# Group 0's feed-forward with seven block products for eight, its weight sums on GpSimd and by DRAM

## The chip, the cores and the metric

The kernel runs on one core of one Trainium2 chip. The metric is the device time of one execution in microseconds, median of the runs shown; less is better. A core has TensorE (PE; PEld is its weight load), VectorE (DVE), ScalarE (ACT), GpSimd (POOL) and SyncE (SP), which issues most DMAs. Each engine works through a queue of its own in order and waits on semaphores.

## The reference, cut to what matters

One encoder layer over two request groups: 1024 new frames of one stream (positions 0 to 1023) and 32 frames of a running stream with 256 cached positions. Model width 1024, feed-forward width D_FF = 2816, all in float32:

```python
    h = x * (1 + sc1) + sh1
    mq, mk, mv, mo, mi, mf, fq, fk, fv, ff, gu, gv = jnp.split(h @ w_in, split_at, axis=-1)
    hm = ...   # mLSTM matrix memory, 4 heads, chunks of 64
    hf = ...   # forgetting attention (FoX), 8 heads of 64, causal
    hg = ...   # gMLP spatial gate
    mix = jnp.concatenate([hm, hf, hg], axis=-1) @ w_o
    x = _layer_norm(ALPHA * x + (1 + g1) * mix, ln1_g, ln1_b)
    h = x * (1 + sc2) + sh2
    y = (jax.nn.silu(h @ w_gate) * (h @ w_up)) @ w_down
    x = _layer_norm(ALPHA * x + (1 + g2) * y, ln2_g, ln2_b)
```

Outputs are both groups' `y`, the new keys, values and forget logs, and the mLSTM states.

## The kernel before, in words

**Columns.** Activations stand feature-major: 128 features a partition, tokens along the columns. The 1056 tokens are cut into two column groups, GN = (512, 544): group 0 is the first 512 prompt tokens, group 1 the other 512 and the 32 sample tokens.

**Precision.** A float32 value is split into a high part (a cast to fp32r on ACT, names ending in `hi` or `h`) and the remainder (a subtraction, mostly on DVE, `lo` or `l`). `gemm` takes three matmuls for each 128 x 128 block: high by high, low activations by high weights, high by low (lines L130, L131, L132). `weights` loads 512 KB as `raw`, casts (L117) and subtracts (L118). There are three `raw` buffers and three of `whi` and `wlo` (RAW, WB).

**Stages.** (1) Input projections and attention for group 0 (to about 350 us); (2) output projection and first LayerNorm of group 0; (3) the feed-forward of group 0, in which `mixers` weave FoX query tiles 4 to 7, mLSTM chunks and the sample stream's attention (about 440 to 835 us); (4) output projection and LayerNorm of group 1; (5) the feed-forward of group 1 (to about 1290 us) and the second LayerNorms. Feed-forward tiles j = 0 to 21 hold 128 of the 2816 features, each with a gate and an up half; GROUPS gathers them in runs of 3, 3, 4, 4, 4, 4, after each of which `down` multiplies by w_down.

**A tile of group 0** (`up`): two weight splits, two products of 8 blocks x 3 matmuls x 512 columns, SiLU as exp, ln, exp on ACT (L1296 to L1298), two products on DVE (L1299, L1300), then the split into `acth` (L1301) and `actl` (L1302).

**A tile of group 1** from SJ = 3 to 20 (`sup`): a Winograd form. The gate and up weights' four quarter blocks (two halves of the 1024 input features for each of gate and up) and the two column halves make a 2 x 2 by 2 x 2 block product, which takes seven block products (u1, x, w3, w4, own, and so on) in place of eight, with sums of weight blocks and sums of activation blocks. Activation sums are made once in `sup_operand` from the LayerNorm's result, stored to DRAM as `dh`. Weight sums come by DRAM too: `sums` copies blocks of w_gu to `dp[j]` (SP's queue) and adds others to it with an accumulating DMA issued by POOL (L1320), a tile ahead. Partial results are put together on DVE (L1395 to L1409).

**Order.** Within an engine a tile scheduler sets the order from the program's dependencies; `weave` and `issue_after` shape it. The FoX score scaling `fox_p` (L924) goes to DVE or ACT by FP. mLSTM scores (L746) take two matmuls of K = 128 per chunk against `mqb`, which holds the queries of two heads with zeros in the other half (memset by POOL, L719). `ln1_pairs` forms the first LayerNorm of group 0 two feature blocks at a time, in `sil`, a tag with two buffers.

## Time and profile before

| | us |
|---|---|
| runs | 1345.75 (1345.29 to 1346.57) |
| profiled execution | 1344.9 (span and whole) |
| PE busy | 1324.0 |
| DVE busy | 989.1 |
| ACT busy | 655.8 |
| POOL busy | 231.9 |

Busy time is the union of an engine's instructions. A PE row's length includes its pipeline, so a matmul's rate is read from the distance of starts. A window line gives, for a stretch of the execution, each engine's busy time and count.

### The profile page before, as it was taken

What the parts mean: (1) busy time and instruction counts of PE and PEld (TensorE: products, weight loads), DVE (VectorE), ACT (ScalarE), POOL (GpSimd) and SP (SyncE); (2) the same over time, 40 slices, a digit from 0 to 9 for tenths busy, and PEclk for the clock granted to TensorE, in tenths of its full rate; (3) what the DMA queues carried; (4) which work ended last, traced back from release to release, by engine and by line L of the source; (5) the groups of instructions that cost most, each with busy time, mean ns of one, the idle gap of its engine ahead of it and who ended that gap; (6) DMA issues with size and microseconds to landing.
All of it is one profiled execution on the core that took longest, in us unless ns stands there. A gap on an engine that the chain in (4) does not pass through costs nothing.

```text
span 1344.9 us, 25607 instructions
## 1 busy us (share of the span) xinstructions
PE 1324.0 (98%) x9684; PEld 1208.3 (90%) x9684; DVE 989.1 (74%) x2091; ACT 655.8 (49%) x1305; POOL 231.9 (17%) x263
## 2 busy tenths in 40 slices
...
GB/s 362 207 299 154 150 204 186 174 131 207 181 195 257 191 136 130 117 163 126 115 121 116 110 104 82 217 175 112 205 231 154 228 148 225 139 175 131 89 79 67
DMA packets 119450, 221.73 MB, mean 165 GB/s; under 512 B 18580, under 2 KB 62768, under 8 KB 119328
## 3 DMA queue, kind: packets, MB, share of 16 engines
...
q14 instruction: 46, 0.38, 0.1%
HBM read 188.13 MB, written 51.85 MB: 178 GB/s over the span
## 4 chain that ended last, share of the span: by engine, by line
PE 68%; DVE 4%; DMA 1%; ACT 1%; issue 1%; DVEq 0%; ACTq 0%
PE up_g L130 6%; PE up_g L132 6%; PE up_g L131 6%; PE dn_g L130 4%; PE dn_g L132 4%; PE dn_g L131 4%; PE sup_u L132 3%; PE sup_u L131 3%; PE sup_u L130 3%; PE wo_g L131 2%; PE wo_g L132 2%; PE wo_g L130 2%; PE sup_g L132 2%; PE sup_g L131 2%; PE sup_g L130 2%; PE fox_t L943 2%
## 5 line engine op out<-in xcount | busy, mean ns | idle before, releaser
L130 PE MATMUL up_g<-tm_ah,up_whi 128*128 128x512 f32 (+1 forms) x384 | 140.0, 365 | 0.0
L131 PE MATMUL up_g<-tm_al,up_whi 128*128 128x512 f32 (+1 forms) x384 | 140.0, 365 | 0.0
L132 PE MATMUL up_g<-tm_ah,up_wlo 128*128 128x512 f32 (+1 forms) x384 | 139.7, 364 | 0.0
L1368 ACT CAST sup_whi<-sup_raw 128x1024 fp32r<-128x1024 f32 x54 | 56.1, 1048 | 89.3 <-PE dn_u L131 43.9
L130 PEld LDWEIGHTS up_g<-tm_ah,up_whi 128*128 128x128 f32 x384 | 72.3, 188 | 11.1 <-DVE tm_al L1246 0.4
L132 PEld LDWEIGHTS up_g<-tm_ah,up_wlo 128*128 128x128 f32 x384 | 72.3, 188 | 11.1
L131 PEld LDWEIGHTS up_g<-tm_al,up_whi 128*128 128x128 f32 x384 | 72.3, 188 | 10.7
L916 ACT ACTIVATE fox_p<-fox_s,fox_fmx 128x384 f32<-128x384 f32 (+2 forms) x96 | 55.2, 579 | 53.0 <-DVE fox_fmx L914 41.2
L1199 DVE SCALAR_TENSOR_TENSOR wo_z<-dn_g,start_mod,wo_z 128x512 f32<-128x512 f32 (+4 forms) x120 | 60.3, 521 | 22.6 <-PE dn_g L132 22.0
L118 DVE TENSOR_TENSOR up_wlo<-up_raw,up_whi 128x1024 fp32r<-128x1024 f32 x50 | 65.2, 1305 | 15.0 <-ACT up_whi L117 13.7
L1369 DVE TENSOR_TENSOR sup_wlo<-sup_raw,sup_whi 128x1024 fp32r<-128x1024 f32 x54 | 68.0, 1263 | 10.7 <-ACT sup_whi L1368 10.7
L117 ACT CAST up_whi<-up_raw 128x1024 fp32r<-128x1024 f32 x50 | 52.4, 1048 | 47.2 <-PE up_g L131 23.9
L130 PE MATMUL dn_g<-up_acth,dn_whi 128*128 128x512 f32 (+2 forms) x200 | 73.5, 368 | 0.8 <-DVE wo_z L1199 0.8
L132 PE MATMUL dn_g<-up_acth,dn_wlo 128*128 128x512 f32 (+2 forms) x200 | 73.3, 366 | 0.0
L131 PE MATMUL dn_g<-up_actl,dn_whi 128*128 128x512 f32 (+2 forms) x200 | 72.8, 365 | 0.0
L948 ACT CAST fox_pth<-fox_t 128x512 fp32r<-128x512 f32 (+1 forms) x80 | 41.6, 542 | 59.2 <-PE fox_t L943 57.5
L117 ACT CAST dn_whi<-dn_raw 128x1024 fp32r<-128x1024 f32 (+1 forms) x44 | 42.7, 971 | 51.7 <-PE up_g L131 16.0
L911 DVE TENSOR_REDUCE fox_fmx<-fox_s 128x1 f32<-128x384 f32 (+2 forms) x96 | 52.8, 553 | 16.3 <-PE fox_s L908 15.0
L949 DVE TENSOR_TENSOR fox_ptl<-fox_t,fox_pth 128x512 fp32r<-128x512 f32 (+1 forms) x80 | 49.9, 631 | 15.9 <-ACT fox_pth L948 15.6
L118 DVE TENSOR_TENSOR dn_wlo<-dn_raw,dn_whi 128x1024 fp32r<-128x1024 f32 (+1 forms) x44 | 49.5, 1125 | 10.4 <-ACT dn_whi L117 9.5
L402 PE MATMUL tm_g<-tm_whi,start_h1h 128*128 128x256 f32 (+1 forms) x192 | 55.3, 288 | 0.7 <-DVE tm_traw L477 0.7
L1320 POOL DMA_DIRECT2D start_dp<-w_gu x19 | 19.8, 1067 | 209.0 <-DMA start_dp<-w_gu 209.0
...
## 6 DMA issues: line engine op xcount, KB each, us to landing
up_raw<-w_gu SPq DMA_DIRECT2D x50, 512.0 KB
ada_late<-w_ada SPq DMA_DIRECT2D x28, 512.0 KB
dn_raw<-w_dn SPq DMA_DIRECT2D x28, 512.0 KB
sup_raw<-w_gu SPq DMA_DIRECT2D x20, 512.0 KB
start_dp<-w_gu SPq DMA_DIRECT2D x19, 512.0 KB
start_dp<-w_gu POOLq DMA_DIRECT2D x19, 512.0 KB, 8.0
wo_raw<-w_o SPq DMA_DIRECT2D x18, 512.0 KB
sup_raw<-start_dp SPq DMA_DIRECT2D x18, 512.0 KB
```

The lines of the kernel that those rows point to most:

```text
L117: nc.scalar.copy(hi[:, :w], raw[:, :w])
L118: (eng or nc.vector).tensor_tensor(lo[:, :w], raw[:, :w], f(hi[:, :w]), ALU.subtract)
L130: nc.tensor.matmul(ps, hi, xh(k), start=start and k == 0, stop=False)
L131: nc.tensor.matmul(ps, hi, xl(k), start=False, stop=False)
L132: self.lastmm = nc.tensor.matmul(ps, lo, xh(k), start=False, stop=stop and k == n - 1)
L402: nc.tensor.matmul(ps[:, :ncol], xh, hi, start=k == 0, stop=False)
L911: nc.vector.tensor_reduce(mxs[:, x:x + 1], s[:, :w], AX.X, ALU.max, negate=True)
L916: nc.scalar.activation(pr[:, lo:hi], banks[x][:, :hi - lo], AF.Exp, bias=mxs[:, 0:1], accum_out=sums[:, x:x + 1])
L949: nc.vector.tensor_tensor(pl[:, :e], ps[:, :e], f(ph[:, :e]), ALU.subtract)
L1199: self.lastz = self.nc.vector.scalar_tensor_tensor(z[:, m, x:y], ps[:, x - a:y - a], g[i], z[:, m, x:y], ALU.mult, ALU.add)
L1368: nc.scalar.copy(h, x)
L1369: tt(l, x, f(h), ALU.subtract)
```

## The change

- Tiles 3 to 17 of group 0 (S0 = 3 up to the last run) use `sup0`, seven block products of 4 blocks x 3 matmuls x 256 columns, 84 matmuls for 48 of 512. Their weight sums `dp` are formed by two additions on POOL, stored to DRAM through POOL's queue, and read by group 1's `sup` for the same tile, so `sums` is left for tiles 18 to 20 alone. The split of w4 (the sums) subtracts on POOL.
- `sup_operand(0, ...)` makes the activation sums between tiles 0, 1 and 2, the block sums on POOL, from group 0's LayerNorm result, which `ln1_pairs` now stores. One block of four is written over the own activations; `own_again` reloads it before tile 18.
- FoX query tiles 4 to 7 are scaled by ACT (FP).
- mLSTM scores use K = 64 rows, four matmuls in two banks (`sts`), and one multiplication of 512 becomes two of 256; `mqb`, its loads and memsets go.
- Smaller buffers: fox `p` for query tiles 4 to 7 sized per tile, pools `pn` and `p2` closed and reopened elsewhere, a DMA scratch of 4096.

```diff
-FP = (0, 0)
+FP = (0, 1)
...
 SJ = 3
+S0 = 3
 TS = 1
...
-        qb = t([P, 2, 2, P], "mqb")
-        nc.gpsimd.memset(qb, 0.0)
-        for a in range(2):
-            r = slice(64 * a, 64 * a + 64)
-            self.load(qb[r, :, a, :L], self.dmqk[r, 0:2, o:o + L])
...
-        st = self.t(self.pss, [P, 512], F32, "s")
+        sts = [self.t(p, [P, 512], F32, x) for p, x in ((self.pss, "s"), (self.pt, "t"))]
         for i in range(2):
-            nc.tensor.matmul(st[:L, 256 * i:256 * i + 256].rearrange("p (a q) -> p a q", a=2)[:, :, :L],
-                             qk[:, 2 + i, :L], qb[:, i, :, :L], start=True, stop=True)
-        nc.vector.tensor_tensor(w[:L, :, :L], st[:L].rearrange("p (h q) -> p h q", h=4)[:, :, :L], w[:L, :, :L], ALU.mult)
+            for a, st in enumerate(sts):
+                r = slice(64 * a, 64 * a + 64)
+                nc.tensor.matmul(st[:L, P * i:P * i + L], qk[r, 2 + i, :L], qk[r, i, :L], start=True, stop=True)
+        for a, st in enumerate(sts):
+            wa = w.rearrange("p (i a) q -> p i a q", a=2)[:L, :, a, :L]
+            nc.vector.tensor_tensor(wa, st[:L, :256].rearrange("p (i q) -> p i q", i=2)[:, :, :L], wa, ALU.mult)
...
-            pr = t([P, W], F32, "p", 4)
+            pr = t([P, W], F32, "p", 4) if i < 4 else t([P, n], F32, f"p{i}", 1)
...
+            self.store(self.dh[0][:, k:k + 2, sl], h)
...
-        if i < FF:
+        if i < FF - TS:
             with self.tc.issue_after(self.lastload.ins):
                 self.store(self.dp[i], blocks(i)[:, 2:3].to_broadcast([P, 2, 512]))
-        if SJ <= i - 1 < FF:
+        if GROUPS[-1][0] <= i - 1 < FF - TS:
             self.nc.gpsimd.dma_start(self.dp[i - 1], blocks(i - 1)[:, 0:4:3], accum_op=ALU.add)
...
+        else:
+            new = lambda tag, w: [self.t(self.px, [P, 4, w], F32R, tag + x, 1) for x in "hl"]
+            q, r, own = new("tx", 2 * n), new("ty", n), [x[0][n][:, 0:4, :n] for x in (self.hh, self.hl)]
+            self.T[c] = [[x[:, :, i:i + n] for x in q] for i in (0, n)] + [r, own]
...
+            tt = (nc.vector if c else nc.gpsimd).tensor_tensor
             tt(y[:, b], y[:, b], x[:, b], ALU.subtract)
             tt(x[:, b], x[:, a], x[:, b], ALU.subtract)
             tt(x[:, a], y[:, b], x[:, a], ALU.add)
             tt(y[:, a], x[:, a], y[:, a], ALU.subtract)
-            for z, (h, l) in zip((x, y), self.T):
+            for z, (h, l) in zip((x, y), pair) if c else ((x, q), (y[:, a], r)):
                 nc.scalar.copy(h[:, k], z)
-                tt(l[:, k], z, f(h[:, k]), ALU.subtract)
+                nc.vector.tensor_tensor(l[:, k], z, f(h[:, k]), ALU.subtract)
...
+        x = self.t(self.px, [P, 1024], F32, "dp", 1).rearrange("p (k n) -> p k n", k=4)
+        self.load(x, self.dh[c][:, 0:4, b])
+        for i, z in enumerate(("w2h", "w2l")):
+            y = f(self.t(self.px, [P, 512], F32R, z, 1)).rearrange("p (k n) -> p k n", k=2)
+            self.load(y, self.dh[c][:, 4 + 2 * i:6 + 2 * i, b])
+            k = slice(2 * i, 2 * i + 2)
+            nc.vector.tensor_tensor(y, y, x[:, k], ALU.subtract)
+            h, l = own
+            nc.scalar.copy(h[:, k], y)
+            nc.vector.tensor_tensor(l[:, k], y, f(h[:, k]), ALU.subtract)
...
+    def sup0(self, j, act, pool):
+        self.phase = "sup"
+        nc = self.nc
+        tt, pp = nc.vector.tensor_tensor, nc.gpsimd.tensor_tensor
+        hh, hl = self.hh[0], self.hl[0]
+        ah, al = act[j] = [self.t(pool, [P, 512], F32R, x, 5) for x in ("acth", "actl")]
+        raw = [self.t(self.wp, [P, 1056], F32, "raw", RAW)[:, :1024] for _ in range(2)]
+        for i in range(2):
+            self.load(raw[i], self.d["w_gu"][j][:, i * 1024:(i + 1) * 1024])
+        lo, hi = slice(0, 512), slice(512, 1024)
+        dp = self.t(self.px, [P, 1024], F32, "dp", 1)
+        pp(dp[:, hi], raw[1][:, lo], raw[1][:, hi], ALU.add)
+        pp(dp[:, lo], raw[1][:, lo], raw[0][:, lo], ALU.add)
+        self.store(self.dp[j].rearrange("p b n -> p (b n)"), dp, nc.gpsimd)
+
+        def split(h, l, x, eng):
+            nc.scalar.copy(h, x)
+            eng(l, x, f(h), ALU.subtract)
+            return [(h[:, k * P:k * P + P], l[:, k * P:k * P + P]) for k in range(x.shape[1] // P)]
+
+        big = lambda x, eng=tt: split(*(self.t(self.wp, [P, 1056], F32R, y, WB)[:, :1024] for y in ("whi", "wlo")), x, eng)
+        w1 = big(raw[0])
+        tt(raw[0][:, lo], raw[0][:, lo], dp[:, hi], ALU.add)
+        tt(raw[0][:, hi], raw[0][:, hi], raw[0][:, lo], ALU.add)
+        w3 = big(raw[0])
+        w4 = big(dp, pp)
+        w2 = split(*(self.t(self.px, [P, 512], F32R, x, 1) for x in ("w2h", "w2l")), raw[1][:, hi], tt)
+        own = lambda t, k0: tuple(lambda k, x=x: x[t][:, k0 + k, :256] for x in (hh, hl))
+        com = lambda i: tuple(lambda k, x=x: x[:, k] for x in self.T[0][i])
+        a, b = slice(0, 256), slice(256, 512)
+        banks = []
+
+        def prod(w, x):
+            if len(banks) % 2 == 0:
+                banks.append(self.t(self.pg, [P, 512], F32, "g"))
+                ps = banks[-1][:, a]
+            else:
+                banks.append(None)
+                ps = banks[-2][:, b]
+            self.gemm(ps, w, slice(0, P), *x)
+            return ps
+
+        u1 = self.t(self.p2, [P, 272], F32, "tmp", 4)[:, :256]
+        x = self.t(self.p2, [P, 544], F32, "sil", 2)[:, :512]
+        uv = self.t(self.px, [P, 512], F32, "uv", 1)
+        nc.scalar.copy(u1, prod(w1[:4], own(0, 0)))
+        tt(x[:, a], prod(w1[4:], own(0, 4)), u1, ALU.add)
+        tt(uv[:, a], u1, prod(w3[:4], com(0)), ALU.subtract)
+        tt(uv[:, b], prod(w4[4:], com(1)), uv[:, a], ALU.add)
+        tt(x[:, b], prod(w3[4:], own(256, 4)), uv[:, b], ALU.add)
+        s = self.t(self.p2, [P, 544], F32, "sil", 2)[:, :512]
+        nc.scalar.activation(s, x, AF.Exp, scale=-1.0)
+        nc.scalar.activation(s, s, AF.Ln, bias=self.one)
+        nc.scalar.activation(s, s, AF.Exp, scale=-1.0)
+        tt(s, x, s, ALU.mult)
+        two = lambda y: y.rearrange("p (t n) -> p t n", t=2)
+        tt(two(uv), prod(w4[:4], com(3)).unsqueeze(1).to_broadcast([P, 2, 256]), two(uv), ALU.add)
+        tt(uv[:, a], prod(w2, com(2)), uv[:, a], ALU.add)
+        nc.vector.scalar_tensor_tensor(uv, uv, -1.0, s, ALU.mult, ALU.mult)
+        nc.scalar.copy(ah, uv)
+        self.lastact = tt(al, uv, f(ah), ALU.subtract)
+
+    def own_again(self):
+        self.phase = "sup"
+        for k in range(4):
+            r = self.t(self.p2, [P, 272], F32, "tmp", 4)[:, :256]
+            self.load(r, self.dh[0][:, k, 256:])
+            h, l = (x[0][256][:, k, :256] for x in (self.hh, self.hl))
+            self.nc.scalar.copy(h, r)
+            self.nc.vector.tensor_tensor(l, r, f(h), ALU.subtract)
...
-        self.nsum = SJ
+        self.nsum = GROUPS[-1][0]
...
+        s6 = ExitStack()
+        self.px = self.pool("px0", ctx=s6)
+        operand = self.sup_operand(0, range(4))
...
+                if S0 <= j < GROUPS[-1][0]:
+                    self.sup0(j, act, pa)
+                    continue
+                if j == GROUPS[-1][0]:
+                    self.own_again()
                 weave(self.up(0, j, act, pa, WIDE if 0 < j < GROUPS[-1][0] else MM[0]))
+                if j < S0:
+                    with tc.issue_after(self.lastact.ins):
+                        next(operand, None)
+                        next(operand, None)
...
+                s6.close()
+                s4.close()
+                self.pn = self.pool("pn", side="right")
...
-    nc = bacc.Bacc("TRN2", target_bir_lowering=False, num_devices=1)
+    nc = bacc.Bacc("TRN2", target_bir_lowering=False, num_devices=1, dynamic_dma_scratch_size=4096)
```

Where the orders of instructions differ, first on DVE near the first changed tile. Before, tile 4's two weight splits (`up_wlo`) among FoX scores (`fox_`) and evacuations of the down product (`wo_z`):

```order
L118 TENSOR_TENSOR up_wlo_8345<-up_raw_8342,up_whi_8344 128x1024
L914 TENSOR_TENSOR fox_fmx_6224<-fox_fmx_6224 128x1
L1199 SCALAR_TENSOR_TENSOR wo_z_883_4902<-dn_g_8290,start_mod_153,wo_z_883_4902 128x512
L919 TENSOR_TENSOR fox_fsm_6225<-fox_fsm_6225 128x1
L920 RECIPROCAL fox_fsm_6225<-fox_fsm_6225 128x1
L1199 SCALAR_TENSOR_TENSOR wo_z_883_4902<-dn_g_8301,start_mod_153,wo_z_883_4902 128x512
L924 TENSOR_SCALAR fox_p_6226<-fox_p_6226,fox_fsm_6225 128x640
L756 TENSOR_TENSOR mlstm_mkw_6245<-mlstm_t_6242,start_col_178 128x256
L118 TENSOR_TENSOR up_wlo_8351<-up_raw_8348,up_whi_8350 128x1024
L911 TENSOR_REDUCE fox_fmx_6247<-fox_s_6250 128x1
L910 TENSOR_TENSOR fox_s_6254<-fox_s_6254,start_maskneg_130 128x128
L911 TENSOR_REDUCE fox_fmx_6247<-fox_s_6254 128x1
```

Now, tile 3: the third sum (`sup_raw<-sup_raw,sup_dp`), w2's split, the fourth sum and w3's split.

```order
L1402 TENSOR_TENSOR sup_raw_8232<-sup_raw_8232,sup_dp_8236 128x512
L910 TENSOR_REDUCE fox_fmx_6012<-fox_s_6019 128x1
L1397 TENSOR_TENSOR sup_w2l_8255<-sup_raw_8233,sup_w2h_8254 128x512
L1403 TENSOR_TENSOR sup_raw_8232<-sup_raw_8232 128x512
L913 TENSOR_TENSOR fox_fmx_6012<-fox_fmx_6012 128x1
L1397 TENSOR_TENSOR sup_wlo_8247<-sup_raw_8232,sup_whi_8246 128x1024
L918 TENSOR_TENSOR fox_fsm_6013<-fox_fsm_6013 128x1
L919 RECIPROCAL fox_fsm_6013<-fox_fsm_6013 128x1
L119 TENSOR_TENSOR dn_wlo_8367<-dn_raw_8364,dn_whi_8366 128x768
L1014 TENSOR_TENSOR foxs_s_6100<-foxs_s_6100,start_smask_139 128x32
L1017 TENSOR_REDUCE foxs_fmx_6110<-foxs_s_6100 128x1
L948 TENSOR_TENSOR fox_ptl_6036<-fox_t_6031,fox_pth_6035 128x384
```

Tile 3's split of w1 (`sup_wlo_8241`) stands earlier in the same queue, the splits and sums of 512 are new, and all of them stand among FoX, sample-stream (`foxs_`) and down work.

On POOL, before, the mixing stage has only the mLSTM work (`mqb` zeros, a column of ones, the output gate's bias):

```order
L719 MEMSET mlstm_mqb_6185 128x512
L724 MEMSET mlstm_mv_1087_6189 128x4
L735 TENSOR_TENSOR mlstm_mo_6192<-mlstm_mo_6192,start_rowp_176 128x256
L719 MEMSET mlstm_mqb_6482 128x512
L724 MEMSET mlstm_mv_1169_6486 128x4
L735 TENSOR_TENSOR mlstm_mo_6489<-mlstm_mo_6489,start_rowp_176 128x256
L719 MEMSET mlstm_mqb_6747 128x512
L724 MEMSET mlstm_mv_1241_6751 128x4
L735 TENSOR_TENSOR mlstm_mo_6754<-mlstm_mo_6754,start_rowp_176 128x256
L719 MEMSET mlstm_mqb_7012 128x512
L724 MEMSET mlstm_mv_1313_7016 128x4
L735 TENSOR_TENSOR mlstm_mo_7019<-mlstm_mo_7019,start_rowp_176 128x256
```

Now, the first changed tiles on POOL, each of them two additions, the store of the sums and w4's split:

```order
L1391 TENSOR_TENSOR sup_dp_8236<-sup_raw_8233 128x512
L1392 TENSOR_TENSOR sup_dp_8236<-sup_raw_8233,sup_raw_8232 128x512
L92 DMA start_dp_14_70<-sup_dp_8236 128x1024
L1397 TENSOR_TENSOR sup_wlo_8251<-sup_dp_8236,sup_whi_8250 128x1024
L1391 TENSOR_TENSOR sup_dp_8482<-sup_raw_8479 128x512
L1392 TENSOR_TENSOR sup_dp_8482<-sup_raw_8479,sup_raw_8478 128x512
L92 DMA start_dp_15_71<-sup_dp_8482 128x1024
L720 MEMSET mlstm_mv_1168_6491 128x4
L1397 TENSOR_TENSOR sup_wlo_8497<-sup_dp_8482,sup_whi_8496 128x1024
L1391 TENSOR_TENSOR sup_dp_8616<-sup_raw_8613 128x512
```

The next tile's sums stand behind w4's split of the tile before, and write the one `dp` buffer that the store reads. 

On PE, the place where tile 4's first product (`up_g`) follows the first down product (`dn_g`), before:

```order
L130 MATMUL dn_g_8329<-up_acth_8084,dn_whi_8314 128x512
L131 MATMUL dn_g_8329<-up_actl_8085,dn_whi_8314 128x512
L132 MATMUL dn_g_8329<-up_acth_8084,dn_wlo_8315 128x512
L130 MATMUL up_g_8354<-tm_ah_4651,up_whi_8344 128x512
L131 MATMUL up_g_8354<-tm_al_4652,up_whi_8344 128x512
L132 MATMUL up_g_8354<-tm_ah_4651,up_wlo_8345 128x512
```

And the same place now:

```order
L131 MATMUL dn_g_8465<-up_acth_8138,dn_whi_8450 128x512
L132 MATMUL dn_g_8465<-up_actl_8139,dn_whi_8450 128x512
L133 MATMUL dn_g_8465<-up_acth_8138,dn_wlo_8451 128x512
L131 MATMUL sup_g_8507<-tm_ah_4651,sup_whi_8486 128x256
L132 MATMUL sup_g_8507<-tm_al_4652,sup_whi_8486 128x256
L133 MATMUL sup_g_8507<-tm_ah_4651,sup_wlo_8487 128x256
```

Each weight block still takes three passes, of 256 columns where there were 512.

58 lines of the change are left out of this document (35 added, 23 removed).

## The prediction

> **What bounds the kernel now.** I read the page's busy line first, then its chain, then windows over the stage that the change touches and, as a yardstick, over the stage of group 1 that already uses seven products.
>
> ```profile
> PE 1324.0 (98%) x9684; PEld 1208.3 (90%) x9684; DVE 989.1 (74%) x2091; ACT 655.8 (49%) x1305; POOL 231.9 (17%) x263
> PE 68%; DVE 4%; DMA 1%; ACT 1%; issue 1%; DVEq 0%; ACTq 0%
> ```
>
> TensorE (PE) is busy 98% of 1344.9 us: only 20.9 us are idle, and the chain that ended last is mostly PE. So time is won only by giving PE less to do, and lost only where another engine becomes late enough to stop it. The windows show how much room the others have (columns: stretch and length, then busy us and count of PE, weight load, VectorE (DVE), ScalarE (ACT), GpSimd (POOL), then granted clock, DMA share and GB/s).
>
> ```profile
> 430.00:476.30 46.30, 46.27 (x301) 40.12 (x301) 34.51 (x72) 30.58 (x65) 11.42 (x11) 1.00 0.66 191
> 476.30:671.00 194.70, 194.70 (x1061) 161.90 (x1060) 142.98 (x302) 95.30 (x201) 4.88 (x10) 1.00 0.48 134
> 671.00:861.20 190.20, 190.20 (x1068) 162.75 (x1067) 131.35 (x267) 93.47 (x192) 11.29 (x9) 1.00 0.42 125
> 950.00:1000.00 50.00, 49.18 (x394) 48.96 (x393) 44.59 (x86) 33.28 (x71) 16.50 (x18) 1.00 0.84 221
> 965.00:990.00 25.00, 24.18 (x193) 23.96 (x192) 24.17 (x50) 18.31 (x37) 3.10 (x3) 1.00 0.90 223
> 990.00:1015.00 25.00, 23.88 (x186) 23.34 (x185) 18.21 (x38) 11.03 (x19) 3.10 (x3) 1.00 0.90 232
> 1050.00:1250.00 200.00, 200.00 (x1594) 199.94 (x1593) 172.01 (x307) 101.11 (x145) 9.27 (x9) 1.00 0.61 173
> 1165.00:1190.00 25.00, 25.00 (x201) 25.00 (x201) 23.77 (x45) 14.43 (x21) 1.03 (x1) 1.00 0.72 215
> 476.28 0.69 DVE L1302 TENSOR_TENSOR up_actl<-up_sil,up_acth 128x512 fp32r<-128x512 f32 x1
> 493.29 0.69 DVE L1302 TENSOR_TENSOR up_actl<-up_sil,up_acth 128x512 fp32r<-128x512 f32 x1
> 643.81 0.68 DVE L1302 TENSOR_TENSOR up_actl<-up_sil,up_acth 128x512 fp32r<-128x512 f32 x1
> ```
>
> In group 0's mixing stage PE is full and DVE is at 73% and 69% of the two halves. L1302 ends a tile: 476.28 is tile 2, 493.29 tile 3, 643.81 tile 10, so the first half holds eight of the changed tiles (3 to 10) and the second seven. In group 1's seven-product stage DVE is at 86% with PE at 100%, and for 25 us (1165 to 1190) DVE reaches 95% (23.77 of 25.00) while PE loses nothing. The change spends DVE and POOL time to save PE time, so the question is whether DVE fits.
>
> **PE's gain.** A changed tile takes 84 matmuls of 256 columns for 48 of 512. PE's rows give starts, not the pipelined lengths:
>
> ```profile
> 464.10 0.40 PE L130 MATMUL up_g<-tm_ah,up_whi 128*128 128x512 f32 x1
> 464.33 0.39 PE L131 MATMUL up_g<-tm_al,up_whi 128*128 128x512 f32 x1
> 440.26 0.28 PE L130 MATMUL up_g<-tm_ah,up_whi 128*128 128x256 f32 x1
> 440.85 0.28 PE L132 MATMUL up_g<-tm_ah,up_wlo 128*128 128x256 f32 x1
> ```
>
> 512 columns start 0.233 us apart over a longer row; 256 columns are (440.85 − 440.26)/5 = 0.118 us apart, each with its own weight load. So 48 × 0.233 = 11.19 us become 84 × 0.118 = 9.95 us: 1.24 us a tile, **−18.6 us** over 15.
>
> **PE's mLSTM scores.** Two fp32 matmuls of 256 columns a chunk (the trace shows four passes) become four of 128 columns on half the rows.
>
> ```profile
> 494.53 0.59 PE L746 MATMUL mlstm_s<-mlstm_mqb,mlstm_mqk 128*128 128x256 f32 x2
> 496.73 0.60 PE L746 MATMUL mlstm_s<-mlstm_mqb,mlstm_mqk 128*128 128x256 f32 x2
> ```
>
> Two passes take 0.60 with 0.38 us of pipeline, so four take about 0.86 us. Eight passes of half the columns take the same if they run one behind the other, and half if two row halves run side by side: between 0 and −0.43 us for each of 8 chunks, 0 to −3.4. No row of before runs on half the array, so I take the middle, **−1.7 us**. [...]
>
> **DMA relief in group 1.** Sixteen pairs of 512 KB copies that form weight sums leave 850 to 1250 us.
>
> ```profile
> 955.60 5.58 DMA start_dh<-lna_tmp
> 992.39 11.37 DMA dn_raw<-w_dn
> ```
>
> These two steps of the chain lie where the DMA engines are 90% busy, and PE loses 0.82 and 1.12 us there (windows 965 and 990). So the gain is 0 to −1.9; I take **−1.0**. Total gain of PE: 18.6 + 1.7 + 1.0 = 21.3 us, to 1323.6.
>
> **DVE's bill.** The prices:
>
> ```profile
> L118 DVE TENSOR_TENSOR up_wlo<-up_raw,up_whi x50: 1207/1225/3076, 421.9 to 977.7; 128x1024 fp32r<-128x1024 f32 x50
> L1300 DVE TENSOR_TENSOR up_sil<-up_g,up_sil x21: 411/692/693, 444.7 to 818.9; 128x512 f32<-128x512 f32 x17, 128x256 f32<-128x256 f32 x4
> L1369 DVE TENSOR_TENSOR sup_w2l<-sup_w,sup_w2h 128x512 fp32r<-128x512 f32 x13 | 8.9, 686 | 0.0
> L924 DVE TENSOR_SCALAR fox_p<-fox_p,fox_fsm x32: 542/682/1049, 457.3 to 816.2; 128x640 f32<-128x640 f32 x8, 128x768 f32<-128x768 f32 x8, 128x896 f32<-128x896 f32 x8, 128x1024 f32<-128x1024 f32 x8
> 836.36 0.69 DVE L1058 TENSOR_TENSOR wo_z<-wo_z,up_pv 128x512 f32<-128x512 f32 x1 [2.21 <-ACT up_pv L1057]
> 836.97 0.74 DVE L1199 SCALAR_TENSOR_TENSOR wo_z<-dn_g,start_mod,wo_z 128x512 f32<-128x512 f32 x1
> ```
>
> A tile had two weight splits at 1.225 and three 512-wide operations at 0.69: 4.52 us, 5 instructions. It gets two splits at 1.225 (w1, w3), three of 512 at 0.686 (w2's split, two block sums), five of 256 at 0.41 (the four early block results and the last), and four of 512 at 0.69: 9.32 us, 14 instructions. Rows that follow each other overlap by 0.08 us (0.69 long, next start 0.61 later), and the windows count that once, so 4.12 becomes 8.20: +4.1 us a tile. The fox scaling goes to ACT: 32 × (0.682 − 0.08) = −19.3, half in each half of the stage. The four reloaded blocks before tile 18 add 4 × 0.42 = 1.7. First half: 142.98 + 8 × 4.1 − 9.6 = 166.2 us of DVE against 194.7 − 8 × 1.24 = 184.8 of PE, 90%. Second: 131.35 + 7 × 4.1 − 9.7 + 1.7 = 152.1 against 181.5, 84%. Like group 1's 86%, this alone would be hidden.
>
> **What POOL does to DVE.** Each changed tile also puts on POOL two sums of 512, a 1024-wide split for w4 and a DMA issue, and POOL does not run beside DVE freely:
>
> ```profile
> L1193 POOL TENSOR_TENSOR wo_z<-wo_z,up_pv x7: 1282/1298/2280, 836.4 to 845.9; 128x512 f32<-128x512 f32 x7
> 836.41 6.55 POOL L1193 TENSOR_TENSOR wo_z<-wo_z,up_pv 128x512 f32<-128x512 f32 x4 [129.93 <-ACT up_pv L1057]
> 272.99 0.59 POOL L91 DMA_DIRECT2D start_dvn<-tm_traw  x1
> 270.65 2.40 POOL L118 TENSOR_TENSOR tm_wlo<-tm_raw,tm_whi 128x1024 fp32r<-128x1024 f32 x1 [0.40 <-ACT tm_whi L117]
> 270.70 2.36 DVE L464 SCALAR_TENSOR_TENSOR tm_brt<-tm_bmv,start_eps,tm_brs 128x1 f32<-128x1 f32 x1 [1.60 <-ACT tm_brs L462]
> 900.34 0.78 POOL L1071 TENSOR_TENSOR wo_zs<-wo_zs,wo_z 128x272 f32<-128x272 f32 x1 [1.12 <-DVE wo_z L1199]
> 900.45 1.75 DVE L118 TENSOR_TENSOR up_wlo<-up_raw,up_whi 128x1024 fp32r<-128x1024 f32 x1 [0.26 <-ACT up_whi L117]
> ```
>
> At 270.70 a DVE operation on one element a lane lasts 2.36 us, until the POOL split that started 0.05 us earlier is over; at 900.45 a 1.22-us split takes 1.75 beside a 0.78-us POOL add; POOL pays too (6.55/4 = 1.64 for 1.28). New POOL arithmetic is 2 × 1.30 + 2.40 = 5.0 us a tile. DVE loses between 0, if it always reads PSUM then, and 5.0, if it always stands. About half of DVE's work in this stage reads two SBUF operands, so I take 2.5 us a tile. [...]
>
> With 2.5 a tile the first half has 166.2 + 20 = 186.2 us of DVE for 184.8 of PE: more than fits. Let DVE use at most 95% of a stretch, as in the window at 1165: 186.2/0.95 = 196.0, a loss of **+11.2 us** for PE. The second half, 152.1 + 17.5 = 169.6, needs 178.5 of 181.5: nothing. Bounds: no contention, 0; PE suffers from 89% on, as in the window at 950 (44.59 of 50, where PE lost 0.82), 209.2 and 190.6, a loss of 24.4 + 9.1 = 33.5.
>
> ACT gets a third 1024 cast, one of 512, one copy (about 1.9 us a tile) and the fox scaling: 188.8 + 28 + 22 = 239 of 366 us, 65%, not a bound.
>
> **The start.** Before tile 0 the second half of LN1 now stores its 256 KB result pairs from a tile with two buffers, so the third and fourth pair wait until the first two have landed. The nearest landing is the 5.58 us on the chain above, against a pair's own work of about 2 us: 0 to 2 × 3.6 = 7.2; PE has no slack there (46.27 of 46.30). Projection matmuls still lie ahead of it in part, so I take **+3 us**. The operand sums (16 of 256 on POOL, 8 splits on DVE, some 5 us) fall on tiles 1 and 2, where DVE has 11 of 46 us free: 0. Smaller buffers: 0, since fox's p tiles get buffers of their own per query block.
>
> **Sum.** 1344.9 − 18.6 − 1.7 − 1.0 + 11.2 + 3 = 1337.8, and the median of the runs stands 0.85 above the profiled execution: I say **1338**. Runs of before spread over 1.3 us; ±0.2% (2.7 us) is about what can be told from no change.
>
> **Rivals.**
> A. *Everything hides.* For it: the 86% of group 1, and the tile scheduler can spread 4.1 us of new work. Against it: POOL is idle in group 1's stage (9.27 of 200) and not here. Time 1344.9 − 21.3 + 0 to 4 = 1324 to 1328. Chance 0.18.
> B. *DVE becomes the bound of the mixing stage.* PE waits for DVE's results (banks to be emptied, w3's split) in both halves, from the point where DVE passes 89%: −21.3 + 33.5 + 3 = +15, 1360. For it: the first half is at 101% by my own terms. If POOL always stands in DVE's way as at 270.70 (5.0 a tile), it is 206.2/0.95 − 184.8 = 32 and 187.1/0.95 − 181.5 = 15, so 47 − 21.3 + 3 = +29, 1374. Against: PE runs at 100% beside 95% in one row. Chance 0.22 in all, mostly 1349 to 1362.
> C. *The chain through POOL decides.* The buffer of the block sums is single: the next tile's sums wait for w4's split (2.40) and for the store to land.
>
> ```profile
> start_dp<-w_gu POOLq DMA_DIRECT2D x19, 512.0 KB, 8.0
> ```
>
> With 2.6 of sums and 8.0 of landing a tile cannot follow sooner than 10.6, and up to 12.2 with POOL at 1.64 an add and 0.59 for the issue, against 9.95 of PE. That bites only where tiles follow each other without down or fox work between; PE's order has five such places: 5 × 2.2 = 11 on top of my sum if nothing overlaps with DVE's wait, 1349. Chance 0.10, half of it within 0.2%.
> D. *256 columns don't run at 0.118 in a long row*, since weight loads bind (PEld is at 199.94 of 200 in group 1): its 1594 matmuls of mostly 272 columns in 200 us are 0.125 each, so at worst 84 × 0.125 = 10.5 us and a gain of 10 instead of 18.6: 1346. Chance 0.03.
>
> **Chances.** The forecast has 0.47, with its own range 1329 to 1346 (contention 1.5 to 3.2 us a tile): 0.40 of it faster by over 0.2%, 0.07 within. A adds 0.18 faster; B 0.18 slower and 0.04 within; C 0.05 within, 0.05 slower; D 0.03 within. That makes 0.58 faster, 0.19 within 0.2%, 0.23 slower. The range 1323 to 1359 reaches from A to B without the full lock.
>
> **What would show it.** Right: PE's busy sum falls by about 20 us; 256-wide starts stay 0.118 apart inside a tile; in the first half DVE stands near 95% and PE's idle rows there name DVE results (sup_wlo, sup_uv, sup_sil); DVE's 1024-wide splits have a mean well over 1.3 us where POOL is busy; a PE gap of some 3 us near tile 0. Wrong: PE without a gap from 480 to 840 (A); PE waiting on POOL's sup_wlo or on store landings (C); gaps in the second half as large as in the first (B); the granted clock below 1.00 in that stage, which no term here holds.

## The result and the profile after

The changed kernel takes 1415.49 us (median; 1414.4 to 1421.89) where the kernel before took 1346.16 beside it: a ratio of 1.053, 95% interval 1.0514 to 1.0547. It is 69 us slower where 8 us of gain were forecast. The page of the changed kernel's profile, its busy line and its chain:

```profile
span 1412.3 us, 27121 instructions
PE 1338.0 (95%) x10260; PEld 1243.6 (88%) x10260; DVE 1074.4 (76%) x2219; ACT 718.3 (51%) x1396; POOL 308.6 (22%) x314
PE 54%; DVE 15%; ACT 4%; DMA 3%; issue 3%; POOL 0%; SPq 0%; DVEq 0%; ACTq 0%; POOLq 0%
```

By the rates of its matmuls PE has 18.6 us less to do in the changed tiles, and yet it is busy 14 us longer in all; 74 us are idle where 20.9 were, and DVE's share of the chain went from 4% to 15%. Two PE rows by tile and form, of before and then of the change, cut the execution in three (each ends with the first and the last start of its group):

```profile
L130 PE MATMUL up_g<-tm_ah,up_whi x384: 277/394/482, 437.7 to 925.8; 128*128 128x512 f32 x136, 128*128 128x256 f32 x56
L130 PE MATMUL wo_g<-up_ah,wo_whi x128: 283/287/361, 856.2 to 904.9; 128*128 128x272 f32 x128
```

```profile
L131 PE MATMUL up_g<-tm_ah,up_whi x144: 277/281/405, 456.1 to 992.8; 128*128 128x256 f32 x112, 128*128 128x512 f32 x32
L131 PE MATMUL wo_g<-up_ah,wo_whi x128: 284/287/487, 923.4 to 972.0; 128*128 128x272 f32 x128
```

| stretch | before | after | difference |
|---|---|---|---|
| start to group 0's first up product | 437.7 | 456.1 | +18.4 |
| that to group 1's output projection ("the stage" below) | 418.5 | 467.3 | +48.8 |
| that to the end | 488.7 | 488.9 | +0.2 |

So two places lost, and one of them lies before the first changed tile. The stage in windows, before and after:

```profile
437.70:856.20 418.50, 418.50 (x2312) 353.49 (x2309) 296.96 (x614) 208.23 (x433) 21.15 (x25) 1.00 0.46 132
```

```profile
456.10:923.40 467.30, 424.42 (x2873) 382.67 (x2870) 382.20 (x741) 272.95 (x531) 119.26 (x97) 0.97 0.48 146
```

PE's work there should be 418.5 − 18.6 = 399.9 us. It stood idle for 467.3 − 424.4 = 42.9 us and was busy 24.5 us longer than its work. The third last column shows a part of why: the mean granted clock (the share of its full clock that PE was given) fell to 0.97. DVE is at 82%, not at 95%. What PE waited for in the stage (us in total, times, longest):

```profile
PE sup_g L131 <- ACT sup_whi L1396: 7.9, 1, 7.9
PE sup_g L131 <- DVE sup_sil L1426: 7.7, 4, 4.1
PE sup_g L131 <- DVE sup_uv L1427: 7.4, 6, 3.0
PE sup_g L131 <- ACT sup_tmp L1425: 4.6, 3, 3.6
PE fox_o L950 <- DVE fox_ptl L948: 3.7, 3, 2.2
PE fox_s L906 <- ACT fox_p L915: 3.3, 2, 2.6
```

L1425, L1426, L1427 and L1428 are the readers of a product: `prod` puts two products into the halves of one bank, and the second one (or the next user of the bank) waits until the first has been read. The longest wait has another origin, which rows of POOL, DVE and ACT show:

```profile
504.94 1.27 POOL L1391 TENSOR_TENSOR sup_dp<-sup_raw 128x512 f32<-128x512 f32 x1 [8.38 <-DVE sup_w2l L1374]
506.17 1.27 POOL L1392 TENSOR_TENSOR sup_dp<-sup_raw,sup_raw 128x512 f32<-128x512 f32 x1
511.19 0.67 DVE L1402 TENSOR_TENSOR sup_raw<-sup_raw,sup_dp 128x512 f32<-128x512 f32 x1
513.70 1.04 ACT L1396 CAST sup_whi<-sup_raw 128x1024 fp32r<-128x1024 f32 x1 [2.72 <-DVE sup_raw L1403]
```

The last step of the activation sums (L1374) and the block sums of a changed tile use the same single `dp` buffer. The first changed tile's sums start only when that step is done and are there at 507.44. DVE, with other work ahead in its queue, takes them up (L1402) only at 511.19, and PE has its operand at 514.79.

Two of these waits also cost more than their length. Around the longest one and around a short one at 782, PE rows in order of time and windows:

```profile
493.37 0.28 PE L131 MATMUL sup_g<-tm_ah,sup_whi 128*128 128x256 f32 x1
493.49 0.28 PE L132 MATMUL sup_g<-tm_al,sup_whi 128*128 128x256 f32 x1
...
514.79 0.58 PE L131 MATMUL sup_g<-up_txh,sup_whi 128*128 128x256 f32 x1 [7.93 <-ACT sup_whi L1396]
515.17 0.42 PE L132 MATMUL sup_g<-up_txl,sup_whi 128*128 128x256 f32 x1
515.39 0.41 PE L131 MATMUL sup_g<-tm_ah,sup_whi 128*128 128x256 f32 x1
515.60 0.41 PE L132 MATMUL sup_g<-tm_al,sup_whi 128*128 128x256 f32 x1
...
782.04 0.63 PE L906 MATMUL fox_s<-fox_k,fox_qp 128*128 128x512 f32 x1 [2.62 <-ACT fox_p L915]
```

```profile
510.00:514.70 4.70, 0.00 (x0) 0.00 (x0) 3.73 (x8) 1.62 (x3) 0.00 (x0) 0.50 0.27 56
514.70:519.20 4.50, 4.41 (x20) 4.41 (x21) 3.20 (x4) 3.81 (x8) 2.45 (x1) 0.50 0.51 158
519.20:523.00 3.80, 3.80 (x49) 2.76 (x48) 1.67 (x6) 1.94 (x5) 0.00 (x0) 0.97 0.57 142
782.00:785.00 3.00, 2.96 (x11) 2.72 (x12) 3.00 (x11) 0.55 (x2) 0.12 (x1) 0.54 0.79 241
```

Matmuls of 256 columns start 0.12 us apart before the stand and 0.21 after it, for 4.5 us, at a granted clock of 0.50: PE pays 7.9 us idle and some 2.2 us more afterwards. The last window follows a wait of only 2.62 us, and its mean clock is 0.54, which costs another 1.4 us.

### The profile page after: what moved, and what is told of

It is laid out like the page before. It is cut to its first block, busy times and chain, and to the rows that moved or that the text cites. A ratio compares the mean times of both kernels' runs of the same rounds, so it can differ in the third digit from the quotient of the medians.

```text
span 1412.3 us, 27121 instructions
## 1 busy us (share of the span) xinstructions
PE 1338.0 (95%) x10260; PEld 1243.6 (88%) x10260; DVE 1074.4 (76%) x2219; ACT 718.3 (51%) x1396; POOL 308.6 (22%) x314
## 4 chain that ended last, share of the span: by engine, by line
PE 54%; DVE 15%; ACT 4%; DMA 3%; issue 3%; POOL 0%; SPq 0%; DVEq 0%; ACTq 0%; POOLq 0%
PE sup_g L131 4%; PE dn_g L131 4%; PE dn_g L132 4%; PE dn_g L133 4%; PE sup_g L133 3%; PE sup_g L132 3%; PE sup_u L133 3%; PE sup_u L132 3%; PE sup_u L131 3%; PE wo_g L131 2%; PE wo_g L133 2%; PE wo_g L132 2%; PE dn_u L131 1%; PE dn_u L132 1%; PE dn_u L133 1%
## 5 line engine op out<-in xcount | busy, mean ns | idle before, releaser
L133 PE MATMUL dn_g<-sup_acth,dn_wlo 128*128 128x512 f32 (+1 forms) x240 | 82.4, 344 | 0.0
L131 PE MATMUL dn_g<-sup_acth,dn_whi 128*128 128x512 f32 (+1 forms) x240 | 82.3, 344 | 0.0
L132 PE MATMUL dn_g<-sup_actl,dn_whi 128*128 128x512 f32 (+1 forms) x240 | 81.7, 341 | 0.0
L131 PE MATMUL sup_g<-tm_ah,sup_whi 128*128 128x256 f32 x240 | 70.2, 292 | 7.3 <-ACT sup_tmp L1425 4.6
L132 PE MATMUL sup_g<-tm_al,sup_whi 128*128 128x256 f32 x240 | 68.5, 285 | 0.0
L133 PE MATMUL sup_g<-tm_ah,sup_wlo 128*128 128x256 f32 x240 | 68.1, 285 | 0.0
L403 PE MATMUL tm_g<-tm_whi,start_ah 128*128 128x256 f32 (+1 forms) x192 | 55.1, 288 | 1.9 <-ACT tm_brs L463 1.9
L405 PE MATMUL tm_g<-tm_whi,start_h1l 128*128 128x256 f32 (+1 forms) x192 | 55.5, 289 | 0.0
L404 PE MATMUL tm_g<-tm_wlo,start_h1h 128*128 128x256 f32 (+1 forms) x192 | 55.4, 288 | 0.0
L131 PEld LDWEIGHTS sup_g<-tm_ah,sup_whi 128*128 128x128 f32 x240 | 45.9, 191 | 10.3 <-ACT sup_tmp L1425 5.7
```

The costliest lines, as they stand in the source:

```text
L131: nc.tensor.matmul(ps, hi, xh(k), start=start and k == 0, stop=False)
L132: nc.tensor.matmul(ps, hi, xl(k), start=False, stop=False)
L133: self.lastmm = nc.tensor.matmul(ps, lo, xh(k), start=False, stop=stop and k == n - 1)
L403: nc.tensor.matmul(ps[:, :ncol], xh, hi, start=k == 0, stop=False)
L404: nc.tensor.matmul(ps[:, :ncol], xh, lo, start=False, stop=False)
L405: self.lastmm = nc.tensor.matmul(ps[:, :ncol], xl, hi, start=False, stop=k == 7)
```

## The experiments

All runs of one batch stand beside runs of the kernel before on the same chip. "Stage" is the stretch defined above, read from the same PE rows.

### The late start

**e1**, the mLSTM scores undone for group 0's own chunks:

```diff
+        old = j < 4
+        if old:
+            qb = t([P, 2, 2, P], "mqb")
+            nc.gpsimd.memset(qb, 0.0)
...
+        if old:
+            st = self.t(self.pss, [P, 512], F32, "s")
...
+        else:
+            sts = [self.t(p, [P, 512], F32, x) for p, x in ((self.pss, "s"), (self.pt, "t"))]
```

> The changed kernel with one part undone: the mLSTM scores of the four chunks of group 0 (the stage before the output projection) are computed as before (zero-padded queries, one bank, two matmuls of 256); the five chunks woven into the feed-forward keep the row-tiled form. Theory 1: the second half of the row-tiled scores goes to a bank of the pool that FoX's transposes use, comes 10 to 18 us after the first half, and lengthens the chain of chunks on which the output projection of group 0 waits. Then the first up product of group 0 starts at about 438 us as before (456.1 in the changed kernel), and the time falls by about 18 us, to about 1397. Rival 1: the late start comes from the smaller buffers and moved pools; then nothing moves (456, 1415).

1394.57 us (1.0369 of before, 1.0339 to 1.0399): 20.9 us less than the changed kernel. The first up product starts at 438.2, the stage is 467.2 as in the changed kernel. So the late start is the scores' alone; buffers, pools and LN1's stores, which this run keeps, have no part in it. (Of the 18.4 us before the first up product in the changed kernel, 10.1 are more idle time of PE; the other 8.3 are busy time, and the clock was 0.50 there for 13.7 us, around 335, 383 and 397.)

**e2**, the kernel before with the row-tiled scores alone (`st` and `qb` replaced by `sts` as in the diff of the change).

> The kernel before with one part of the change alone: row-tiled mLSTM scores in two banks for all chunks. Theory 1: the first up product moves from 437.7 to about 456, and the time rises by about 18 us to about 1364; if the feed-forward stage suffers too, a little more. Rival 1 (buffers and pools cause the late start): no later start, and 0 to 3 us gained, 1343 to 1346.

1371.14 us (1.0195, 1.0165 to 1.0224): 26 us lost by this part alone, more than expected. The first up product is at 458.3 (+20.6) and the stage at 421.8 (+3.3).

**e8**, e2 with both halves in the score pool:

```diff
-        sts = [self.t(p, [P, 512], F32, x) for p, x in ((self.pss, "s"), (self.pt, "t"))]
+        sts = [self.t(p, [P, 512], F32, x) for p, x in ((self.pss, "s"), (self.pss, "s"))]
```

> The kernel before with row-tiled scores, but both halves in the two banks of the score pool, none in the pool that the FoX transposes use. Theory 1 (the second half waits for a transpose bank): the halves follow each other at once, the first up product is back at 438 to 442 us (458.3 with the second half in the transposes' pool), time 1344 to 1350. Rival: taking two banks for one chunk is what costs, whichever pool they come from, since FoX's scores then wait for theirs; the first up product stays at 450 or later, time 1358 or more.

1354.91 us (1.0068, 1.0055 to 1.0082), above the expected range by 5; the first up product at 441.2, within it, and the stage 419.2. The profiled execution took 1351.84, so some 3 of the median's 9 us over before are in no profile. The bank of the second half is the main cause, but not all of it; what the rest is stays open. PE's score rows of the first chunk in the kernel before, then of the first and fourth chunk in the changed kernel, then of the first and of a woven chunk in e8:

```profile
239.95 1.03 PE L746 MATMUL mlstm_s<-mlstm_mqb,mlstm_mqk 128*128 128x256 f32 x4
```

```profile
238.30 0.71 PE L744 MATMUL mlstm_s<-mlstm_mqk 64*128 64x128 f32 x4
254.56 0.71 PE L744 MATMUL mlstm_t<-mlstm_mqk 64*128 64x128 f32 x4
...
344.13 0.71 PE L744 MATMUL mlstm_s<-mlstm_mqk 64*128 64x128 f32 x4
362.83 0.71 PE L744 MATMUL mlstm_t<-mlstm_mqk 64*128 64x128 f32 x4
385.37 1.01 PE L131 MATMUL wo_g<-tm_ah,wo_whi 128*128 128x256 f32 x3 [5.89 <-ACT tm_ah L1130]
```

```profile
239.10 0.71 PE L743 MATMUL mlstm_s<-mlstm_mqk 64*128 64x128 f32 x4
242.23 0.71 PE L743 MATMUL mlstm_s<-mlstm_mqk 64*128 64x128 f32 x4
...
630.66 0.72 PE L743 MATMUL mlstm_s<-mlstm_mqk 64*128 64x128 f32 x8
```

In the changed kernel the second half (`mlstm_t`) runs 16.3 us after the first, and in the fourth chunk 18.7 us after it, since it needs a bank of the pool that transposes use. A chunk goes on only when both are there; the fourth ends the chain, and the output projection of group 0 stands 5.89 us for its operand at 385. In e8 the first chunk's halves are 3.1 us apart. Nor do the halves save PE time in the changed kernel: 2 × 0.71 us for 1.03, since there they never run side by side. They can: in e8's woven chunk at 630.66 all eight passes together take 0.72 us, as long as one half alone.

### The stage

**e3**, a bank for each product:

```diff
-            if len(banks) % 2 == 0:
-                banks.append(self.t(self.pg, [P, 512], F32, "g"))
-                ps = banks[-1][:, a]
-            else:
-                banks.append(None)
-                ps = banks[-2][:, b]
+            ps = self.t(self.pg, [P, 512], F32, "g")[:, a]
```

> The changed kernel, but each of the seven products of a group-0 tile takes a PSUM bank of its own in place of half a bank. Theory 2: in the changed kernel the second product of a bank waits until the first one has been read by ACT or DVE, so PE stands (25 us of its waits are on those readers), and its granted clock falls behind each longer stand. Then the stage from the first up product to the output projection of group 1 (467 us in the changed kernel) falls by 20 to 45 us, the mean clock rises from 0.98 to 0.99 or more, and the time is 1370 to 1395. Rival 2: DVE, slowed by POOL, is what PE waits for whichever bank it writes; then the stage falls by less than 10 us, time 1405 to 1415.

1399.12 us (1.0403, 1.0373 to 1.0433), 16 less than the changed kernel; the stage is 452.0 (−15.3). Less than theory 2 wanted and more than rival 2; the mean clock of the execution, which theory 2 wanted at 0.99, stayed at 0.98.

**e4**, constants in place of POOL's reads:

```diff
-        pp(dp[:, hi], raw[1][:, lo], raw[1][:, hi], ALU.add)
-        pp(dp[:, lo], raw[1][:, lo], raw[0][:, lo], ALU.add)
+        nc.gpsimd.memset(dp[:, hi], 0.01)
+        nc.gpsimd.memset(dp[:, lo], 0.01)
...
+            if eng is pp:
+                nc.gpsimd.memset(f(l), 0.0)
```

> The changed kernel, with POOL's two block sums per tile and its subtraction for w4 replaced by constants written by POOL into the same tiles: the sums and the low part of w4 are left out, so DVE meets no POOL instruction that reads SBUF there. Rival 2 (DVE loses to POOL): DVE's two-operand instructions fall to their undisturbed length (weight splits 1.42 to 1.22 us, the last products 1.12 and 0.91 to 0.69), 25 to 30 us of DVE time are freed, and the time falls by 20 us or more, to about 1390. Theory 2 (waits on readers of a shared bank): DVE gets shorter but PE keeps most of its waits, and the time falls by less than 10 us.

1386.04 us (1.0305, 1.0268 to 1.0342), 29 less than the changed kernel; the stage is 438.8 (−28.5). The time is as rival 2 had it. But constants also take POOL's arithmetic out of the chain ahead of the products, so this run alone doesn't tell the two apart; e6 was made for that. Two groups of DVE in the changed kernel's stage, and its splits by line (shortest/median/longest); then the same in e4, and e4's window:

```profile
L1397 DVE TENSOR_TENSOR sup_wlo<-sup_raw,sup_whi 128x1024 fp32r<-128x1024 f32 x30 | 42.6, 1419 | 7.2 <-ACT sup_whi L1396 6.8
L1438 DVE SCALAR_TENSOR_TENSOR sup_uv<-sup_uv,sup_sil 128x512 f32<-128x512 f32 x15 | 16.7, 1116 | 0.1
...
L1397 DVE TENSOR_TENSOR sup_wlo<-sup_raw,sup_whi x30: 1195/1224/2639, 485.3 to 862.7; 128x1024 fp32r<-128x1024 f32 x30
```

```profile
L1441 DVE SCALAR_TENSOR_TENSOR sup_uv<-sup_uv,sup_sil 128x512 f32<-128x512 f32 x15 | 10.2, 682 | 0.1
...
L1400 DVE TENSOR_TENSOR sup_wlo<-sup_raw,sup_whi x30: 1201/1215/1228, 484.6 to 833.3; 128x1024 fp32r<-128x1024 f32 x30
456.00:895.00 439.00, 414.80 (x2872) 376.74 (x2872) 347.05 (x738) 271.90 (x532) 66.13 (x97) 0.98 0.51 154
```

The longest split is 1.228 us where it was 2.639 in the changed kernel, the last operation on `sup_uv` has a mean of 0.682 for 1.116, and DVE is busy 347.1 for 382.2 us: 35 us, or 2.3 a tile, were time in which POOL held it. POOL still writes as often; only its reads are gone.

**e6**, POOL's three operations of a tile on DVE (`tt = pp = nc.vector.tensor_tensor`).

> The changed kernel with POOL's three operations of a tile (two block sums, the low part of w4) on DVE, everything computed. It separates the two things that writing constants instead had removed together: DVE blocked beside POOL's reads, and POOL's slow chain (2.6 us of sums, 2.4 us of w4) ahead of the products. DVE gets 15 x (2 x 0.69 + 1.22) = 39 us of work more and loses no time to POOL (about 28 us in the changed kernel). If blocking and DVE's occupancy are the cost, the two nearly cancel: 1410 to 1430. If POOL's slow chain is the cost, PE gains: 1385 to 1400. DVE's weight splits must fall to a mean of 1.22 us either way.

1405.23 us (1.0432, 1.0341 to 1.0524), between the two ranges. The stage is 461.9 (−5.4), DVE's splits have a median of 1.216, and its busy time in the stage is 376.6 for 382.2: the work moved to it is about what it got back. So of e4's 28.5 us, DVE's time and POOL's chain can't be priced one by one.

**e5**, FoX's scaling back on DVE (`FP = (0, 0)`).

> The changed kernel with FoX's scaling of query tiles 4 to 7 back on DVE (32 instructions, 0.99 us each on ACT in the changed kernel, 0.68 on DVE before). If DVE's occupancy in the feed-forward stage (82% of 467 us) is what PE pays for, 19 us more of DVE cost 8 to 19 us: 1423 to 1434. If ACT's queue is the late one (PE waited 4.9 us on FoX's scaled rows from ACT), it gains up to 8 us: 1407 to 1415.

1419.47 us (1.0538, 1.0466 to 1.061), between the two ranges, and the interval holds the changed kernel's ratio. In the profiled execution (1422.47; the other took 1416.48) the stage is 475.7 (+8.4) with DVE busy 401.2 us: the direction of the first theory, but by the two times it can't be told from no change.

**e9** and **e10**, nothing of the seven products, and the activation sums alone (`S0 = 18`, no `own_again`; e9 without the calls of `operand`, e10 with them up to the own blocks; both with the scores as in e1).

> The changed kernel with group 0's own chunks scored as before and without seven products, activation sums and reload in group 0 (all its tiles take the eight products, the weight sums of tiles 3 to 20 go by DRAM as before). What is left of the change: LN1's stores, FoX's scaling on ACT and its smaller buffers, row-tiled scores in the five woven chunks. If the stage's loss belongs to the seven products, its length (first up product to the output projection of group 1) is 418 to 425 us against 418.5 before, and the time is 1345 to 1353. If FoX's scaling on ACT and single buffers stop PE by themselves, the stage is 430 us or more and the time 1358 or more.

> The kernel of e9 with group 0's activation sums made between tiles 0, 1 and 2 as in the changed kernel (16 sums of 256 on POOL, 8 splits on DVE, 8 casts on ACT, loads of the stored LayerNorm), but used by nothing. I had priced this at 0. In the run with tiles 11 to 17 PE lost 7.8 us of idle time and ran at a clock of 0.87 between 463 and 513 us, where only this preparation is new. If it is the cause, this run is 10 to 15 us longer than e9; if the loads or LN1's stores in e9 are, the two are within 3 us.

1349.68 us (1.0026, 1.0014 to 1.0038) and 1351.55 (1.005, 1.0034 to 1.0065). Both of e9's figures are those of its first case: the stage's loss belongs to the seven products. Its stage is 423.8: 5.3 over before, most of which e2 showed (3.3, the scores of the woven chunks). e9's first up product is at 437.0, so LN1's stores cost nothing. e10's stage is 426.0, 2.2 more than e9: the activation sums by themselves are not what stopped PE; the case of 10 to 15 us did not come.

**e7**, seven products in tiles 11 to 17, own banks, scores as in e1, POOL's arithmetic kept. The activation sums' last step ran before tile 3, so tiles 3 to 10 multiplied some blocks of sums in place of activations: the same work with other values.

> Seven products in tiles 11 to 17 only (the weight sums of tiles 3 to 10 by DRAM as before), each product in its own bank, and the scores of group 0's own chunks as before. The loss of the stage is 49 us for 15 tiles, 33 with own banks, so 2.2 a tile net of the gain. If it is spread evenly, seven tiles leave the stage at about 418.5 + 7 x 2.2 = 434 us and the time at about 1361. If it grows faster than the number of tiles because DVE only fills up with many of them (my bill had the second half at 94% and the first at 101%), the stage is at 410 to 420 and the time 1337 to 1348.

1367.19 us (1.015, 1.0101 to 1.0199), stage 438.7: neither guess (434, or 410 to 420). Half of the loss fell between 463 and 513 us, where the activation sums were made beside FoX, and PE was full from 513 to 688, where there are no changed tiles.

### Versions meant to be better

b1 to b7 have the scores as before throughout, weight sums by DRAM for both groups (`sums` called from two tiles ahead of the first changed one, as group 1 does), all arithmetic on DVE, and own banks, b5 apart:

```diff
-        for i in range(2):
-            self.load(raw[i], self.d["w_gu"][j][:, i * 1024:(i + 1) * 1024])
...
+        self.load(raw[0], self.d["w_gu"][j][:, :1024])
+        self.load(dp, self.dp[j].rearrange("p b n -> p (b n)"))
+        self.load(w2r, self.d["w_gu"][j][:, 1536:])
...
+STEPS = {4: 1, 5: 1, 6: 1, 7: 1, 8: 1, 10: 1}    # b1: activation sums, one step a tile
```

> A version meant to beat both: seven products in tiles 11 to 17 of group 0, weight sums by DRAM for both groups (no arithmetic on POOL), w4's low part and the activation sums on DVE, a PSUM bank per product, the activation sums spread over tiles 4 to 8 and 10, mLSTM scores as before throughout. Gain 7 x 1.24 = 8.7 us of PE; DVE gets 7 x (4.1 + 1.22) + 7 = 44 us in the stage less 19 for FoX's scaling, with no loss to POOL, so it stays near 80%. If POOL's blocking, the shared banks and the late scores are the whole loss: stage 410 to 414, time 1337 to 1342. If latency between DVE's results and PE costs even then (three banks only): stage 418 to 428, time 1346 to 1356.

> The same version with all of tiles 3 to 17 and the activation sums between tiles 0, 1 and 2. DVE in the stage: 297 + 15 x 5.3 + 7 - 19 = 365 us of 400 of PE work, 91%, with nothing lost to POOL. If only POOL's blocking and the shared banks made PE stand, the stage comes to 400 to 410 and the time to 1327 to 1338. If a DVE so full is late for PE by itself, the stage stays at 430 or more (438.8 with constants in place of POOL's reads) and the time at 1357 or more.

> As b1 and b2 (weight sums by DRAM, no arithmetic on POOL, own banks, scores as before), but seven products in tiles 6 to 17 and one step of the activation sums in each of tiles 0 to 5. PE's work in the stage is 418.5 - 12 x 1.24 = 403.6 us. If b2's rest (36.6 us over its 400 of work) lies at the crowded start, the stage is 408 to 414 and the time 1335 to 1342, better than before. If it is spread over the changed tiles (2.4 us each), it is 12 x 2.4 = 29 over, 430 to 434, time 1356 to 1362.

> As b3 with seven products in tiles 8 to 17 and the activation sums in tiles 1 to 5 and 7. PE's work in the stage: 418.5 - 10 x 1.24 = 406.1. If the rest lies at the start: 410 to 415, time 1336 to 1343. If spread: 406.1 + 24 = 430, 1356.

> b2 (seven products in tiles 3 to 17, no arithmetic on POOL, scores as before) with two products to a bank, as in the changed kernel. If waiting for a bank's first reader costs PE by itself, the stage is 10 to 20 us longer than b2's 436.6. If it only cost because POOL held DVE up, it is within 4 us of b2.

> b1 (seven products in tiles 11 to 17, weight sums by DRAM, own banks, scores as before) with FoX's scaling of query tiles 4 to 7 on DVE as before. If DVE's room decides, 19 us more of DVE make the stage 3 to 8 us longer than b1's 415.4, time 1347 to 1353. If ACT's queue is what PE waits for, it is 2 to 4 us shorter, time 1339 to 1343.

> b1 with seven products in tiles 14 to 17 only. PE's work in the stage: 418.5 - 5.0 = 413.5. If DVE's room decides, these four, where FoX thins out, lose next to nothing: 413 to 415, time 1341 to 1344. If every changed tile costs about 0.8 us as in b1, it is 416 to 417 and the time 1345 to 1346.

| run | changed tiles | us | ratio, interval | stage | PE's work | over |
|---|---|---|---|---|---|---|
| b2 | 3 to 17 | 1363.16 | 1.0131 (1.0106 to 1.0156) | 436.6 | 399.9 | 36.7 |
| b5, shared banks | 3 to 17 | 1380.45 | 1.0252 (1.023 to 1.0273) | 454.5 | 399.9 | 54.6 |
| b3 | 6 to 17 | 1349.71 | 1.0022 (1.0008 to 1.0036) | 419.2 | 403.6 | 15.6 |
| b4 | 8 to 17 | 1348.71 | 1.0021 (1.0011 to 1.0031) | 420.2 | 406.1 | 14.1 |
| b1 | 11 to 17 | 1344.85 | 0.9991 (0.998 to 1.0003) | 415.4 | 409.8 | 5.6 |
| b6, FoX scaling on DVE | 11 to 17 | 1354.04 | 1.0056 (1.0035 to 1.0077) | 415.3 | 409.8 | 5.5 |
| b7 | 14 to 17 | 1351.96 | 1.0047 (1.0029 to 1.0065) | 416.0 | 413.5 | 2.5 |

"PE's work" is 418.5 less 1.24 for each changed tile. b2 came out in its second case and b5 in its first; b1, b3 and b4 lie between their two. None is faster than the kernel before by more than can be told. b1's stage is 3 us shorter, and 2.6 of them are given back in the output projection that follows.

b5 against b2 settles the banks: without any arithmetic on POOL, sharing them still costs 17.9 us of the stage. b2, the cleanest version with all 15 tiles, has these windows (the stage, two stretches at its start, and one in its middle):

```profile
438.00:870.00 432.00, 409.91 (x2813) 373.94 (x2812) 357.05 (x758) 265.64 (x521) 36.47 (x41) 0.97 0.67 188
463.00:488.00 25.00, 21.17 (x106) 17.58 (x105) 19.18 (x43) 14.78 (x28) 2.76 (x3) 0.86 0.72 203
488.00:513.00 25.00, 16.13 (x111) 14.14 (x111) 16.20 (x39) 9.64 (x22) 2.04 (x3) 0.73 1.02 254
613.00:638.00 25.00, 25.00 (x206) 24.81 (x205) 24.86 (x53) 20.50 (x40) 3.37 (x3) 1.00 0.64 187
```

At the start 12.7 us are idle and the clock is at 0.86 and 0.73 with DVE at only 77% and 65%: there PE waits for a chain (the longest two gaps, 6.30 and 3.60 us, are FoX's output waiting for `fox_ptl`), not for a full DVE. At 613 DVE is at 99% and PE loses nothing. In these two stretches PE is busy for 16 us at a clock of 0.50 (480.8 to 491.1 and 501.3 to 511.6), which costs 8. Idle time and clock together take 12.7 + 8.0 = 20.7 us, and b3, which drops that start, is 21 us less over than b2. The other 15.6 us of b3 (14.1 in b4) lie in the tiles that are left: more than the one expectation allowed for them, and less than the even price of the other. In b3 11.5 us of it are idle time, in several waits of which the longest is 2.4 us, with the clock at 1.00.

b6's stage is b1's, in neither of its cases; b7's is at the low end of its second case. Both missed the time, since the projection after the stage took longer. From the first product of group 1's output projection to group 1's first up product it is 96.4 us before, 99.0 in b1, 103.8 in b7, 107.7 in b6. PE rows of b6 there, and the whole stretch before and in b6:

```profile
859.86 0.59 PE L132 MATMUL wo_g<-up_ah,wo_whi 128*128 128x272 f32 x1 [1.68 <-ACT up_ah L1141]
861.67 0.59 PE L133 MATMUL wo_g<-up_al,wo_whi 128*128 128x272 f32 x1 [1.21 <-DVE up_al L1142]
```

```profile
856.20:952.60 96.40, 96.40 (x782) 95.89 (x781) 79.33 (x143) 48.66 (x102) 53.90 (x55) 1.00 0.54 151
853.20:960.90 107.70, 102.15 (x781) 99.53 (x781) 88.60 (x152) 50.33 (x106) 60.32 (x60) 0.94 0.55 157
```

PE waits for the casts and splits of that projection's operand, which are made from the last mixing results. Of b6's 11.3 us more, 5.6 are idle time; the rest is longer busy time at a mean clock of 0.94. Why these operands come late in b6 and b7 and hardly in b1 stays open. That a shorter stage runs into the end of the mixing work is only a reading of these rows; no run varied it alone.

## Why the prediction was wrong, point by point

- **PE's gain of 18.6 us.** Right as far as the rows go: 256 columns start 0.12 us apart in the changed tiles too (493.37 and 493.49). (84 × 0.118 is 9.91 and not 9.95, half a microsecond in 15 tiles.)
- **"PE's mLSTM scores … between 0 and −0.43 us for each of 8 chunks".** This failed first. The sum priced two matmuls and left out the bank: the change takes a second one, from a pool that other work holds, in a chain of chunks that the output projection waits for. It cost 18.4 us at the start, 20.6 in e2. The gain itself was below 0 in the changed kernel (0.71 twice for 1.03), outside the term's range: the sum had all eight passes in one place. e8 shows that case where its halves meet (eight passes in 0.72 us); in the changed kernel none meet.
- **DVE's bill.** The work was sized rightly: 15 × 4.1 − 19.3 + 1.7 + 37.5 = 81 us more were predicted for the stage, 85 are there. POOL's hold was put at 2.5 us a tile, by a halving that no row had shown, though rows stood at both ends: at 270.70 DVE stood until POOL's split was over, and at 836.97, beside the POOL row of 836.41, its operation that reads the bank `dn_g` took 0.74 us, where the mean of that operation in the stage is 0.75. The hold measures 2.3 (e4), not the 5.0 of a whole hold, which the prediction's range calls the full lock.
- **"Let DVE use at most 95% of a stretch, as in the window at 1165".** This is the step that failed most. It made the loss 11.2 us; measured are 467.3 − 399.9 = 67 us over PE's work, with DVE at 82%. The yardstick, group 1's stage, is built otherwise: each product there takes a bank of its own, out of two pools of three, and no FoX or mLSTM chain runs beside it. PE is stopped by single results that come late: its waits name them, and b2 loses at its start with DVE at 65 to 77% and nothing at 99%. DVE's time still counts through them, as e4 shows. How the 67 us divide is known only in part: b2, without shared banks, POOL's arithmetic and the new scores, is still 36.7 over, some 21 of it at the start; the causes of the rest were not taken apart. My bounds, 0 to 33.5, were drawn from the same idea, so the range missed too.
- **The waits that the change adds.** Two products to a bank was in the diff and in no term of mine: 15.3 us in the changed kernel (e3), 17.9 without POOL (b5 against b2). POOL's arithmetic: 28.5 (e4), of which the sum had a part as DVE time. The two overlap, so they are not added here.
- **The clock.** I named it only as something no term held. In the stage it was 0.50 for 30.7 us in six stretches (the longest from 509.2 to 519.4), and PE was busy for 22.2 of these, so it took some 11 of the 24.5 us by which PE was busy beyond its work; the longer scores took 3 (e2). The other 10 no run accounts for.
- **Start of LN1, +3; activation sums, 0; DMA relief, −1.** LN1's stores cost nothing (e9). The sums alone cost 2.2 us (e10 against e9). Beside changed tiles they cost more: by the rows, the wait of 7.93 us comes from the `dp` buffer that their last step holds and from DVE's queue behind it, and no term had that; no run varied this alone. The last stretch moved by 0.2 us, so the relief gave nothing.
- **Rivals.** B, DVE as the bound of the mixing stage, had the side and the place, but not the mechanism or the price (1360). C named POOL's chain and the single buffer of the sums, and that buffer has a part in the largest wait, but for the first changed tile only and for the activation sums' sake, not for a store's landing. Slower had a chance of 0.23, and no case of mine held both places.
